# Scores of the 64-feature heads as products of row halves of the array, and small products gathered

## The chip, the cores and the metric

The kernel runs on one NeuronCore of one Trainium2 chip. A time is the device time of one execution in microseconds (us). The profile records one execution. It names the engines PE (TensorE, matrix products) with PEld (its loads of the stationary operand), DVE (VectorE), ACT (ScalarE), POOL (GpSimd) and SP (SyncE, which here issues the loads of weights). The array of TensorE has 128 rows, along which the sum of a product runs, and 128 columns.

## What is computed

`x` is 256 positions by 1024 features, float32. Block 1 runs two layers of FFN1, hybrid mixer and FFN2, each with a residual and a layer norm; block 2 runs two layers of a second mixer. Only the mixers contain what the change touches:

```python
# block 1: hybrid_mixer, head dimension 64
qa, ka, va, qr, kr, vr, gr = jnp.split(x @ w_in, IN_SPLITS, axis=-1)
y_attn = sliding_window_sink_attention(rope(qa), rope(ka), va, sinks)  # 8 query heads, 2 key heads, window 128
y_ret = multiscale_retention(rot(qr), rot(kr) / 8, vr, gr)             # 8 heads, decay per head
return jnp.concatenate([y_attn, y_ret], axis=-1) @ w_out
# block 2: second_block
o_a = mla_attention(qa_nope, qa_rope, ka_nope, ka_rope, va)            # 6 heads, 64+32 features, causal
o_b = dilated_attention(p_qb, p_kb, p_vb, slopes_b)                    # 6 heads, 64 features
o_c = sparse_attention(p_qc, p_kc, p_vc, p_qi, p_ki, p_wi, slopes_c)   # 4 heads, 64 features
#   index score of a key: sum over 8 heads of w * relu(q_idx . k_idx); each query keeps its best 64 keys
sub = (jnp.concatenate([o_a, o_b, o_c], -1) * silu(p_gate)) @ w_out
```

## The kernel before

`program` runs the stages `Ffn1`, `Mixer1`, `Ffn2` twice and `Mixer2` twice. Weights stream once from memory through a ring of six stage buffers on SP's one queue. Every piece is split into a high and a low part (`whi` by a copy on ACT, L300; `wlo` by a subtraction on DVE, L302), and a projection makes three products per 128 features with them (`mm<-whi,xx`, `mm<-wlo,xx`, and transposed, with the activations as what streams, `mm<-xx,whi`). Scores, values and transposes are plain float32; each shows as two records on PE. All matrix products go through the helper `mm` (L331), transposes through `transposes` (L446), and so they are told apart by their tiles: `ac` (four PSUM banks: scores, values, retention), `mm` (two banks: projections), `tr` (two banks: transposes).

**Scores.** The features lie on the rows of the array. A head has 64 features, and the transposed activations hold two heads, one in rows 0 to 63 and one in rows 64 to 127. Before, one operand of each product is a copy padded with zeros in the other head's rows, and the product uses all 128 rows: `kz` (keys of the window attention), `qrz` (queries of the retention), `kiz` (index keys), `kcz` (keys of c), `kbz` (keys of b). POOL fills the zeros, and the two halves are copied by two instructions. Attention a of `Mixer2` has 96 features and uses 96 rows.

**From scores to values.** `softmax` (L657) brings a bank of scores, one (128 x 512) tile of several heads, to `P`: on DVE a scaled addition of the bias (L661), the maximum (L666, L668), small steps for the sinks (L669 to L678), the reciprocal (L679) and in `Mixer1` the product with it (L808); on ACT one exponential per head (L672). `pT` (L682) transposes the blocks of `P` on PE and copies them to `PT` on ACT (L690) or DVE (L692); `av` multiplies them with the values, two heads at a time in column halves of the array (rows of the profile with `128*64`). In the retention, `ret_s` (L839) makes scores of pairs of heads and multiplies them by the decay on DVE (L851, tile `S`); `ret_av` multiplies `S` with the values (`ac<-vr,S`).

**Order.** A scheduler works the order out once, when the kernel is built: it takes the instructions in the order in which the program writes them as their rank, and fixes for each engine one list that the engine works through in order. On the chip a waiting instruction holds back all that stand behind it on its engine. `Mixer1.body` and `Mixer2.body` write scores, transposes, values and projections in alternation, so that a softmax runs on DVE and ACT while PE does a projection. One layer pair has 6 score units of the window attention in `Mixer1` (two of 4 heads x 128 keys, four of 2 heads x 256 keys), 6 of the retention, and in `Mixer2` 5 units of a, 3 of c, 5 of b and two calls of `choose` (the index scores and the selection of keys).

## Time and profile before

| what | value |
|---|---|
| time, median of three runs | 1356.9 us (1353.8, 1356.9, 1357.55) |
| time of the profiled execution | 1357.66 us |
| its span, from first to last instruction | 1355.9 us |
| granted clock of TensorE, mean | 0.997 |
| busy: PE / DVE / ACT / POOL | 98% / 76% / 55% / 3% |
| matrix products (PE records) | 7654 |
| FFN1, `Mixer1`, FFN2 of layer 0 | about 15 to 205, 205 to 306, 306 to 500 us |
| FFN1, `Mixer1`, FFN2 of layer 1 | about 504 to 700, 700 to 802, 802 to 997 us |
| `Mixer2`, layers 0 and 1 | about 997 to 1170, 1178 to 1350 us |

A busy share is the mean over stages with different work. In the timeline a row merges neighbouring instructions of one kind: its start, the time from the first one's start to the last one's end, the engine, the line, what is written and read, the rows*columns of the array for PE, the shape, and the number of records. A PE record's end is modelled and reaches beyond the start of the next, so the time that a group takes is read from its start to the start of what comes behind it. A bracket says for how long the engine stood before the row, and what ended that.

### The profile page before, as it was taken

The page shows a single profiled execution, that of the slowest core. Times are in us where ns is not written, and L with a number is a line of the kernel's source. Part 1 is how long each engine was busy: PE and PEld are TensorE (multiplying, and loading weights), DVE is VectorE, ACT ScalarE, POOL GpSimd, SP SyncE. Part 2 cuts the span into 40 slices and gives each one's busy share as a digit, 9 for nine tenths or more (in the row PEclk, how much of TensorE's full clock was granted, in tenths as well). Part 3 has the DMA queues.
Part 4 walks back from the last instruction along what each step waited for, and adds up shares of the span by engine and source line. Part 5 has one row for each costly group of instructions (what it writes and reads, how often), then busy time and mean ns, then how long its engine had stood idle before and what let it go on. Part 6 is the DMA issues. An engine that isn't in the chain of part 4 may idle for free.

```text
span 1355.9 us, 20444 instructions
## 1 busy us (share of the span) xinstructions
PE 1334.9 (98%) x7654; PEld 1149.7 (85%) x7654; DVE 1035.4 (76%) x1705; ACT 752.2 (55%) x1324; POOL 37.2 (3%) x55
## 2 busy tenths in 40 slices
PE   9999999999999999999999999999999999999997
PEld 7888888888888888878888878888889989799896
DVE  7876769878977669777579778687585796866976
ACT  7655535455654546545445456555355678366691
POOL 0000010010000000000010110000010000000000
PEclk9999999999999999999999999999999999999999
DMA  9987625446877628877433647687445435365320
GB/s 320 343 285 250 218 63 175 154 138 249 310 247 259 218 82 313 282 261 240 147 109 125 209 149 267 204 271 251 129 152 190 144 101 163 127 194 167 121 98 31
DMA packets 75236, 262.89 MB, mean 194 GB/s; under 512 B 9168, under 2 KB 9552, under 8 KB 75008
## 3 DMA queue, kind: packets, MB, share of 16 engines
q1 hardware_dynamic: 74592, 259.82, 57.3%
q0 software_dynamic: 544, 1.75, 0.4%
q8 instruction: 60, 0.98, 0.3%
q14 instruction: 40, 0.33, 0.1%
HBM read 260.49 MB, written 1.05 MB: 193 GB/s over the span
## 4 chain that ended last, share of the span: by engine, by line
PE 82%; DVE 9%; DMA 4%; issue 2%; ACT 2%; POOL 0%; SPq 0%; DVEq 0%; ACTq 0%; POOLq 0%
PE mm L331 39%; PE ac L331 27%; PE tr L331 12%; DMA st<-in_w 4%; PE tr L446 3%; DVE wlo L302 2%; DVE xlo L302 1%; DVE x L411 1%; ACT whi L300 0%; DVE xx L378 0%; DVE ada L317 0%; POOL rs_y L389 0%; DVE bn L414 0%; DVE x L437 0%; DVE x L438 0%
## 5 line engine op out<-in xcount | busy, mean ns | idle before, releaser
L302 DVE TENSOR_TENSOR wlo<-st,whi 128x1024 fp32r<-128x1024 f32 (+4 forms) x319 | 373.1, 1179 | 81.5 <-ACT whi L300 80.4
L300 ACT ACTIVATE whi<-st 128x1024 fp32r<-128x1024 f32 (+4 forms) x319 | 324.0, 1022 | 125.1 <-PE mm L331 57.1
L331 PE MATMUL mm<-xx,whi 128*128 128x256 f32 (+1 forms) x1296 | 334.0, 333 | 0.6 <-ACT whi L300 0.6
L331 PE MATMUL mm<-xx,wlo 128*128 128x256 f32 x928 | 261.2, 282 | 0.0
L331 PEld LDWEIGHTS mm<-xx,whi 128*128 128x128 f32 x1296 | 220.4, 190 | 24.7 <-ACT whi L300 0.9
L331 PE MATMUL mm<-whi,xx 128*128 128x512 f32 (+3 forms) x744 | 220.8, 373 | 0.6 <-DVE xx L378 0.4
L331 PE MATMUL tr<-xx,whi 128*128 128x512 f32 x560 | 195.9, 392 | 0.8 <-ACT whi L300 0.8
L331 PEld LDWEIGHTS mm<-xx,wlo 128*128 128x128 f32 x928 | 176.0, 190 | 2.1 <-DVE wlo L302 0.8
L331 PE MATMUL tr<-xx,wlo 128*128 128x256 f32 x560 | 156.6, 280 | 0.5 <-DVE wlo L302 0.5
L331 PEld LDWEIGHTS mm<-whi,xx 128*128 128x128 f32 x744 | 135.5, 188 | 24.3 <-issue 1.4
L300 ACT ACTIVATE xhi<-st 128x1024 fp32r<-128x1024 f32 x106 | 110.5, 1058 | 74.4 <-PE ac L331 63.0
L302 DVE TENSOR_TENSOR xlo<-st,xhi 128x1024 fp32r<-128x1024 f32 x106 | 128.6, 1220 | 25.2 <-ACT xhi L300 24.4
L331 PE MATMUL mm<-wlo,xx 128*128 128x512 f32 (+3 forms) x372 | 137.9, 371 | 0.0
L331 PE MATMUL ac<-xlo,hth 128*128 128x512 f32 x320 | 126.7, 396 | 0.0
L331 PE MATMUL ac<-xhi,hth 128*128 128x512 f32 x320 | 125.8, 393 | 0.0
L331 PEld LDWEIGHTS tr<-xx,whi 128*128 128x128 f32 x560 | 104.7, 187 | 24.2 <-ACT whi L300 1.1
L331 PEld LDWEIGHTS tr<-xx,wlo 128*128 128x128 f32 x560 | 105.6, 189 | 2.2 <-DVE wlo L302 1.0
L331 PE MATMUL ac<-xhi,htl 128*128 128x512 f32 x320 | 105.5, 394 | 0.0
L317 DVE SCALAR_TENSOR_TENSOR ada<-st,sc,ada 128x1024 f32<-128x1024 f32 x42 | 53.9, 1283 | 37.0 <-DMA st<-in_w 36.7
L331 PEld LDWEIGHTS mm<-wlo,xx 128*128 128x128 f32 x372 | 70.1, 188 | 10.4
L331 PEld LDWEIGHTS ac<-xhi,hth 128*128 128x128 f32 x320 | 60.3, 188 | 14.1
L331 PEld LDWEIGHTS ac<-xhi,htl 128*128 128x128 f32 x320 | 60.2, 189 | 12.4
(286 smaller groups left out, 1890.2 us busy)
## 6 DMA issues: line engine op xcount, KB each, us to landing
st<-in_w SPq DMA_DIRECT2D x442, 512.0 KB, 4.5
st<-in_w SPq DMA_DIRECT2D x20, 384.0 KB, 3.5
g<-in_lng SPq DMA_DIRECT2D x8, 512.0 KB, 4.9
b<-in_lnb SPq DMA_DIRECT2D x8, 512.0 KB, 4.8
st<-in_w SPq DMA_DIRECT2D x8, 432.0 KB, 3.9
st<-in_w SPq DMA_DIRECT2D x8, 296.0 KB, 4.1
st<-in_xT SPq DMA_DIRECT2D x4, 256.0 KB, 3.9
x<-in_x SPq DMA_DIRECT2D x2, 512.0 KB, 6.8
```

What stands on the lines that cost most here:

```text
L300: nc.scalar.activation(out=hi[:, :m], in_=st[:, :m], func=AF.Copy)
L302: nc.vector.tensor_tensor(out=lo[:, :m], in0=st[:, :m], in1=hi[:, :m].bitcast(F32), op=ALU.subtract)
L317: nc.vector.scalar_tensor_tensor(out=self.ada, in0=st, scalar=c, in1=self.ada, op0=ALU.mult, op1=ALU.add)
L331: self.nc.tensor.matmul(*a, **k)
L411: nc.vector.scalar_tensor_tensor(out=x[:, c0:c1], in0=x[:, c0:c1], scalar=alpha, in1=src, op0=ALU.mult, op1=ALU.add)
L446: self.nc.tensor.transpose(ps[:m, 128 * i:128 * i + 128], s, self.idn)
```

## The change

The padded copies and their zeros go. One copy of the whole pair takes the place of two half copies, and each product of a 64-feature head names rows 0 to 63 or rows 64 to 127 for both its operands. The units are made in pairs, one for each row half, into two PSUM banks, and the products of the two halves alternate: in the window attention units 0 and 1, 2 and 4, 3 and 5; in the retention the even and the odd heads; in `choose` the even and odd index heads; in c and b the even and odd heads (`make` with `halves=True`; the units of c are now two, one of 4 heads x 128 keys and one of 4 heads x 256 keys; of b three, the first with 6 heads x 128 keys). Attention a stays in 96 rows. b runs six softmaxes in place of five, c four in place of three, since each bank has its own.

The second part moves work. `together` and `ready` first make the transposes and copies of several units and then the value products of these units in a row; a scheduler's mark (`issue_after`) keeps the products behind the first one of the row. `pT` makes up to four blocks per bank, and its copies alternate between DVE and ACT by a count. The body of `Mixer2` is written in another order, with some of the value products inside and behind the gate projection (`mid`). There are three `PT` buffers in `Mixer2` in place of two. Per layer pair there are nine calls of `together` or `ready`: three in `Mixer1`, six in `Mixer2`.

```diff
+        out = []
+        for i in range(0, len(blocks), 4):
+            bs = blocks[i:i + 4]
+            ps = K.transposes(bs)
+            T = self.scr.tile([128, 512], F32, tag="PT", name="PT", bufs=self.pt_bufs)
+            m = 128 * len(bs)
+            self.n_pt += 1
+            if self.n_pt % 2 == 0:
+                nc.scalar.activation(out=T[:, :m], in_=ps[:, :m], func=AF.Copy)
+            else:
+                nc.vector.tensor_copy(out=T[:, :m], in_=ps[:, :m])
+            out += [T[:, 128 * j:128 * j + 128] for j in range(len(bs))]
+        return out
...
+        fs = [f() for f in steps]
+
+        def products():
+            first = None
+            for f in reversed(fs):
+                with self.K.tc.issue_after(first) if first is not None else nullcontext():
+                    ins = f()
+                first = first if first is not None else ins
+        return products
...
-        self.qT, self.kz = t("qT", [4, 256], self.keep), t("kz", [2, 256])
-        self.qrz, self.krT = t("qrz", [8, 256], self.keep), t("krT", [4, 256], self.keep)
+        self.qT, self.kT = t("qT", [4, 256], self.keep), t("kT", [256])
+        self.qrT, self.krT = t("qrT", [4, 256], self.keep), t("krT", [4, 256], self.keep)
...
+        def score(*two):
+
+            pvs = []
+            for i in two:
+                t, h0, nh, nk = self.attn_units()[i]
+                pvs.append(K.bank("ac", 4)[:, :nh * nk].rearrange("p (h n) -> p h n", h=nh))
...
-            pv = ps[:, :nh * nk].rearrange("p (h n) -> p h n", h=nh)
...
-                h = h0 + j
-                K.mm(pv[:, j, :], lhsT=self.qT[:, h % 4, ts], rhs=self.kz[:, h // 4, :nk], start=True, stop=True)
+                for i, pv in zip(two, pvs):
+                    h = self.attn_units()[i][1] + j
+                    r = slice(64 * (h // 4), 64 * (h // 4) + 64)
+                    K.mm(pv[:, j, :], lhsT=self.qT[r, h % 4, ts], rhs=self.kT[r, :nk], start=True, stop=True)
...
+                t, h0, nh, nk = self.attn_units()[i]
+                p = st.pop(i)
+                nt = nk // 128
+                T = self.pT([p[:, h, 128 * j:128 * j + 128] for h in range(nh) for j in range(nt)])
...
+                        for kt in range(nt):
+                            for e in range(2):
+                                with K.tc.issue_after(first) if first is not None else nullcontext():
+                                    ins = K.mm(y[64 * e:64 * e + 64, c:c + 128], lhsT=self.v[:, kt, 64 * g:64 * g + 64],
+                                               rhs=T[(j + e) * nt + kt], start=kt == 0, stop=kt == nt - 1)
...
+            nc.vector.tensor_copy(out=self.qrT[:, :, ts], in_=ps.rearrange("p (a n) -> p a n", a=4))
...
-            ps = K.bank("ac", 4)
...
-                     start=True, stop=True)
...
+            pvs = [K.bank("ac", 4)[:, :np * nq].rearrange("p (h n) -> p h n", h=np) for _ in range(2)]
+            for j in range(np):
+                for e in range(2):
+                    r = slice(64 * e, 64 * e + 64)
+                    K.mm(pvs[e][:, j, :], lhsT=self.krT[r, p0 + j, 128 * kt:128 * kt + 128], rhs=self.qrT[r, p0 + j, 128 * kt:],
+                         start=True, stop=True)
+            dec = K.dec.rearrange("p (a e n) -> p e a n", e=2, n=256)
+            for e in range(2):
+                P = scr.tile([128, 512], F32, tag="P", name="S", bufs=self.p_bufs)
+                sv = P[:, :np * nq].rearrange("p (h n) -> p h n", h=np)
+                nc.vector.tensor_tensor(out=sv, in0=pvs[e], in1=dec[:, e, p0:p0 + np, :nq], op=ALU.mult)
+                for j in range(np):
+                    S[2 * (p0 + j) + e, kt] = sv[:, j, :]
...
-        score(0)
-        score(1)
+        score(0, 1)
+        score(2, 4)
         self.proj(2, 0, lambda ps: self.rot(ps, 512, 1, 0, "qr"))
-        av(0)
-        score(2)
+        self.together(av(0), av(1))
+        score(3, 5)
         self.proj(2, 1, lambda ps: self.rot(ps, 512, 1, 1, "qr"))
-        av(1)
-        score(3)
         self.proj(3, 0, lambda ps: self.rot(ps, 512, 2, 0, "kr"))
-        av(2)
-        score(4)
+        self.together(av(2), av(4))
         ret_T(0)
         self.proj(3, 1, lambda ps: self.rot(ps, 512, 2, 1, "kr"))
-        av(3)
-        score(5)
+        self.together(av(3), av(5))
         self.proj(4, 0, vcopy(0))
         ret_T(1)
-        av(4)
-        av(5)
         self.proj(4, 1, vcopy(1))
         K.affine(1, self.l, last)
         ret_s(1, 0, 4)
-        ret_s(1, 4, 4)
-        for j in range(4):
-            ret_s(0, 2 * j, 2)
+        ret_s(0, 0, 2)
+        ret_s(0, 2, 2)
...
     p_bufs = 5
-    pt_bufs = 2
+    pt_bufs = 3
...
+        self.kcT, self.kiT = kk[:, 0:2], kk[:, 2]
+        self.kr, self.wi = (kk[:, 3, c:c + 2 * n].rearrange("p (t n) -> p t n", t=2) for c, n in ((0, 32), (64, 8)))
...
-        for h0 in range(0, 8, nh):
-            ps = K.bank("ac", 4)
+        for p0 in range(0, 4, nh):
+            ps = [K.bank("ac", 4) for _ in range(2)]
             for j in range(nh):
-                h = h0 + j
-                K.mm(ps[:, nk * j:nk * j + nk], lhsT=qiT[:, h // 2, 128 * t:128 * t + 128], rhs=self.kiz[:, h % 2, :nk],
-                     start=True, stop=True)
-            rl = self.rl[:, (h0 // nh) % 2]
-            nc.scalar.activation(out=rl, in_=ps, func=AF.Relu, scale=0.125)
-            for j in range(nh):
...
+                for e in range(2):
+                    r = slice(64 * e, 64 * e + 64)
+                    K.mm(ps[e][:, nk * j:nk * j + nk], lhsT=qiT[r, p0 + j, 128 * t:128 * t + 128], rhs=self.kiT[r, :nk],
+                         start=True, stop=True)
...
+            if halves:
+                for p0 in range(0, nh // 2, n):
+                    ps = range(p0, min(p0 + n, nh // 2))
+                    us.append((t, 128 + 128 * t, [[2 * p + e for p in ps] for e in range(2)]))
...
+            t, nk, banks = us[i]
+            pvs = [K.bank("ac", 4)[:, :len(hs) * nk].rearrange("p (h n) -> p h n", h=len(hs)) for hs in banks]
+            for j in range(len(banks[0])):
+                for pv, hs in zip(pvs, banks):
+                    K.mm(pv[:, j, :], lhsT=q(hs[j], slice(128 * t, 128 * t + 128)), rhs=k(hs[j], nk), start=True, stop=True)
...
+                    for h in sorted(ps)[::2]:
...
+                        for kt in range(nt):
+                            for e in range(2):
+                                with K.tc.issue_after(first) if first is not None else nullcontext():
+                                    ins = K.mm(y[64 * e:64 * e + 64, c:c + 128], lhsT=v[:, kt, c + 64 * e:c + 64 * e + 64],
+                                               rhs=T[h + e, kt], start=kt == 0, stop=kt == nt - 1)
+                                first = first if first is not None else ins
...
-                if g == 0:
-                    gated(k)
...
-        a_av(0)
+        self.together(a_av(0), a_av(1))
...
-        a_av(1)
+        a_score(3)
         self.choose(1, self.qiT)
-        a_score(3)
-        a_av(2)
         a_score(4)
-        kbz = scr.tile([128, 6, 256], F32, tag="kT", name="kbz")
-        self.zero_halves(kbz)
-        bv = kbz.rearrange("p (a b) n -> p a b n", b=2)
+        kbT = scr.tile([128, 3, 256], F32, tag="kT", name="kbT")
 
         def post6(b, ps):
             n = 2 - b
-            pv = ps[:, :256 * n].rearrange("p (a n) -> p a n", a=n)
-            self.copy(0, bv[0:64, 2 * b:2 * b + n, 0, :], pv[0:64])
-            self.copy(1, bv[64:128, 2 * b:2 * b + n, 1, :], pv[64:128])
+            self.copy(b, kbT[:, 2 * b:2 * b + n, :], ps[:, :256 * n].rearrange("p (a n) -> p a n", a=n))
 
         self.proj_T(3, post6)
-        a_av(3)
+        self.together(a_av(2), a_av(3))
         c_score(0)
-        a_av(4)
-        c_score(1)
-        c_av(0)
-        c_score(2)
+        b_score, b_av = self.make(6, 0.125, half(qbT), keys(kbT), vb, 5, self.alibi(0, lambda t: self.seg(K.lc, t)), True)
         self.proj(post7)
         K.affine(3, self.l, last)
-        c_av(1)
-        b_score, b_av, nbu = self.make(6, 0.125, lambda h, s: qbT[:, h // 2, s], lambda h, nk: kbz[:, h, :nk],
-                                       vb, 5, self.alibi(0, lambda t: self.seg(K.lc, t)))
-        c_av(2)
+        self.together(a_av(4), c_av(0))
+        c_score(1)
         b_score(0)
+        go = []
+        self.proj_T(4, gpost(0), lambda: go.append(self.ready(c_av(1))))
+        go.pop()()
+        go.append(self.ready(b_av(0)))
         b_score(1)
         b_score(2)
-        b_av(0)
-        b_score(3)
-        b_av(1)
-        b_score(4)
-        self.proj_T(4, gpost(0))
-        b_av(2)
+        gated(0)
+        gated(1)
...
-        self.proj_T(4, gpost(1))
+        go.pop()()
+        self.proj_T(4, gpost(1), lambda: go.append(self.ready(b_av(1), b_av(2))))
...
+        go.pop()()
```

On PE, at the first scores of `Mixer1`, before (`ro`, `rk` are the rotated queries and keys, `P` a softmax):

```order
L446 MATMUL tr<-idn,ro 128x128 x4
L446 MATMUL tr<-idn,rk 128x128
L331 MATMUL ac<-kz,qT 128x128 x8
L331 MATMUL mm<-whi,xx 128x512
L331 MATMUL mm<-wlo,xx 128x512
```

and after:

```order
L446 MATMUL tr<-idn,ro 128x128 x4
L446 MATMUL tr<-idn,rk 128x128
L331 MATMUL ac<-kT,qT 128x128 x8
L331 MATMUL ac<-kT,qT 128x256 x4
L331 MATMUL mm<-whi,xx 128x512 x2
L331 MATMUL mm<-wlo,xx 128x512
```

The first half of the 256-key scores now stands directly behind the 128-key scores.

On DVE, at the same place, before:

```order
L748 COPY kz<-tr 64x128 x2
L661 SCALAR_TENSOR_TENSOR P<-ac,win 128x512
L302 TENSOR_TENSOR wlo<-st,whi 128x1024
L668 TENSOR_REDUCE nm<-P 128x4
L661 SCALAR_TENSOR_TENSOR P<-ac,win 128x512
L669 TENSOR_TENSOR nm<-nm,sink 128x4
L302 TENSOR_TENSOR wlo<-st,whi 128x1024
L670 TENSOR_SCALAR nm<-nm 128x4
L668 TENSOR_REDUCE nm<-P 128x4
L676 TENSOR_TENSOR es<-sink,nm 128x4
```

and after:

```order
L766 COPY kT<-tr 128x128
L302 TENSOR_TENSOR wlo<-st,whi 128x1024
L660 SCALAR_TENSOR_TENSOR P<-ac,win 128x512 x2
L667 TENSOR_REDUCE nm<-P 128x4 x2
L668 TENSOR_TENSOR nm<-nm,sink 128x4
L660 SCALAR_TENSOR_TENSOR P<-ac,win 128x512
L669 TENSOR_SCALAR nm<-nm 128x4
L668 TENSOR_TENSOR nm<-nm,sink 128x4
L667 TENSOR_REDUCE nm<-P 128x2
L675 TENSOR_TENSOR es<-sink,nm 128x4
```

The steps of the two first softmaxes and of a third one (over two heads) now alternate, with no weight split between them.

On PE, at the retention (`krT`, `vr` are its keys and values), before:

```order
L446 MATMUL tr<-idn,P 128x128 x4
L331 MATMUL ac<-qrz,krT 128x128 x6
L331 MATMUL ac<-PT,v 64x128 x4
L331 MATMUL ac<-qrz,krT 128x128 x2
L331 MATMUL ac<-qrz,krT 128x256 x8
L331 MATMUL ac<-vr,S 128x64 x6
L331 MATMUL mm<-whi,xx 128x512
L331 MATMUL ac<-vr,S 128x64 x2
```

and after:

```order
L331 MATMUL mm<-whi,xx 128x512
L331 MATMUL ac<-qrT,krT 128x128 x8
L331 MATMUL ac<-qrT,krT 128x256 x8
L331 MATMUL ac<-vr,S 128x64 x5
L331 MATMUL mm<-whi,xx 128x512
L331 MATMUL mm<-wlo,xx 128x512
L331 MATMUL mm<-whi,xx 128x512
L331 MATMUL ac<-vr,S 128x64 x3
```

The 16 scores now stand in one row, with no window values between them.

On PE, at c and b in `Mixer2` (`vc` are the values of c, `va` those of a, `kk` holds the keys of c and of the index), before:

```order
L331 MATMUL ac<-PT,vc 64x128 x4
L331 MATMUL ac<-kbz,qbT 128x128 x3
L446 MATMUL tr<-idn,P 128x128 x2
L331 MATMUL ac<-kbz,qbT 128x128
L446 MATMUL tr<-idn,P 128x128 x2
L331 MATMUL ac<-kbz,qbT 128x128 x2
L331 MATMUL ac<-kbz,qbT 128x256
L331 MATMUL ac<-PT,vc 64x128 x4
L331 MATMUL ac<-kbz,qbT 128x256
L331 MATMUL mm<-xx,whi 128x256
```

and after:

```order
L331 MATMUL mm<-xx,whi 128x256 x2
L331 MATMUL mm<-xx,wlo 128x256
L331 MATMUL ac<-PT,vc 64x128 x4
L331 MATMUL ac<-PT,va 64x128 x4
L331 MATMUL ac<-kk,qcT 128x256 x4
L331 MATMUL ac<-kbT,qbT 128x128 x6
L331 MATMUL mm<-xx,whi 128x256 x2
```

Four kinds of small work that alternated stand in two rows: values, then scores.

## Rows read from the trace of the kernel before

**Rows 1.** The page: the span, and the busy time of each engine.

```profile
span 1355.9 us, 20444 instructions
...
PE 1334.9 (98%) x7654; PEld 1149.7 (85%) x7654; DVE 1035.4 (76%) x1705; ACT 752.2 (55%) x1324; POOL 37.2 (3%) x55
```

**Rows 2.** Windows: stretch; length; busy us of PE, PEld, DVE, ACT, POOL; clock, DMA.

```profile
215.00:260.00 45.00, 44.98 (x248) 35.96 (x247) 42.97 (x87) 25.49 (x61) 0.00 (x0) 1.00 0.50 161
...
1074.00:1122.00 48.00, 47.19 (x354) 42.69 (x353) 46.64 (x126) 36.10 (x93) 1.47 (x2) 1.00 0.37 123
1122.00:1140.00 18.00, 18.00 (x150) 16.73 (x149) 9.39 (x15) 17.19 (x34) 0.00 (x0) 1.00 0.36 119
```

**Rows 3.** Timeline of PE: the first scores of Mixer1, and what follows them.

```profile
214.33 1.95 PE L331 MATMUL ac<-kz,qT 128*128 128x128 f32 x16
...
216.04 0.47 PE L331 MATMUL mm<-whi,xx 128*128 128x512 f32 x1
```

**Rows 4.** Timeline of PE: the index scores of both halves, and what follows each.

```profile
1064.70 1.95 PE L331 MATMUL ac<-kiz,qiT 128*128 128x128 f32 x16
1066.40 0.36 PE L331 MATMUL mm<-xx,wlo 128*128 128x256 f32 x1
...
1080.65 3.72 PE L331 MATMUL ac<-kiz,qiT 128*128 128x256 f32 x16
1084.21 1.03 PE L331 MATMUL ac<-kaT,qaT 96*128 96x256 f32 x4
```

**Rows 5.** Timeline of PE: values in column halves, between whole-array products.

```profile
227.74 0.40 PE L331 MATMUL mm<-wlo,xx 128*128 128x512 f32 x1
...
228.07 0.66 PE L331 MATMUL ac<-PT,v 128*64 128x128 f32 x8
...
228.66 1.13 PE L331 MATMUL ac<-kz,qT 128*128 128x256 f32 x4
...
229.63 0.60 PE L446 MATMUL tr<-idn,P 128*128 128x128 f32 x4
```

**Rows 6.** Timeline of PE: projection products, one behind the other.

```profile
258.43 0.62 PE L331 MATMUL mm<-whi,xx 128*128 128x512 f32 x2
258.89 0.39 PE L331 MATMUL mm<-wlo,xx 128*128 128x512 f32 x1
```

**Rows 7.** Timeline of DVE: steps one behind the other, then the two first softmax ends.

```profile
217.16 0.68 DVE L668 TENSOR_REDUCE nm<-P 128x4 f32<-128x512 f32 x1
...
217.76 0.68 DVE L661 SCALAR_TENSOR_TENSOR P<-ac,win 128x512 f32<-128x512 f32 x1
...
218.36 0.15 DVE L669 TENSOR_TENSOR nm<-nm,sink 128x4 f32<-128x4 f32 x1
218.43 1.22 DVE L302 TENSOR_TENSOR wlo<-st,whi 128x1024 fp32r<-128x1024 f32 x1
...
219.56 0.16 DVE L670 TENSOR_SCALAR nm<-nm 128x4 f32<-128x4 f32 x1
...
224.94 0.69 DVE L808 TENSOR_TENSOR P<-P,rd 128x512 f32<-128x512 f32 x1
...
227.41 0.68 DVE L808 TENSOR_TENSOR P<-P,rd 128x512 f32<-128x512 f32 x1
```

**Rows 8.** Timeline of PE: transposes of the first softmax of Mixer1.

```profile
225.92 0.60 PE L446 MATMUL tr<-idn,P 128*128 128x128 f32 x4
```

**Rows 9.** Timeline of PE: end of the retention.

```profile
261.80 4.17 PE L331 MATMUL ac<-qrz,krT 128*128 128x128 f32 x20
265.81 1.45 PE L331 MATMUL ac<-vr,S 128*128 128x64 f32 x12
267.06 0.48 PE L331 MATMUL mm<-whi,xx 128*128 128x512 f32 x1
```

**Rows 10.** Timeline of DVE: one of the six decay products of the retention.

```profile
263.42 0.69 DVE L851 TENSOR_TENSOR S<-ac,dec 128x512 f32<-128x512 f32 x1 [0.17 <-PE ac L331]
```

**Rows 11.** Timeline of PE: a wait for copied transposes in Mixer2.

```profile
1086.68 0.66 PE L331 MATMUL ac<-PT,va 128*64 128x128 f32 x8 [0.29 <-ACT PT L690]
```

More of the change, by code (lines that the diff above doesn't have):

```diff
@@ L745, in qk_T @@
         ps = K.transposes([self.ro["k", t][:, 0:128]])
[L746 to L748 removed]
+        nc.vector.tensor_copy(out=self.kT[:, ts], in_=ps[:, 0:128])
     def first(self, t, g):
@@ L1068, in make @@
+    def make(self, nh, scale, q, k, v, k0, bias, halves):
         K, nc = self.K, self.K.nc
[L1069 to L1070 removed]
+        us = self.units(nh, halves)
         st, yps = {}, {}
         def score(i):
[L1074 to L1082 removed]
```

243 lines of the change are left out of this document (109 added, 134 removed).

## The prediction

> **What bounds the kernel now.** I read the page first, for which engine has no idle time; then the busy time by windows over the mixers, since the change touches nothing else; then PE's timeline at each kind of product that changes; and last the rows of DVE there, because DVE makes the operands that PE takes next. The page shows PE busy for 1334.9 of 1355.9 us [rows 1], so the time is what PE has to do, plus 21 us of start, end and waits. In the two stretches with most of the small products PE is busy for 44.98 of 45.0 us and 47.19 of 48.0 us. But DVE is busy for 42.97 and 46.64 us of the same stretches, so only 2.0 and 1.4 us are free on it, while it has 9.39 of 18 us behind the second one [rows 2]. A microsecond taken from PE counts there only if DVE can follow. The granted clock is 1.00 in all these stretches [rows 2].
>
> A unit's price comes from starts, since ends are modelled. Sixteen records of 128 columns run from 214.33 to 216.04: 1.71 us, 0.107 each, eight products [rows 3]. The index scores give 1.70 us for the same shape and, for eight products of 256 columns, 3.56 us, of which about 0.11 is the step into the group: 3.45 us, or 0.216 a record [rows 4]. A projection product of 512 columns takes 0.23 us [rows 6].
>
> **The change part by part.**
>
> *Row halves.* Two products of 64 rows that run beside each other take the time of one. In `Mixer1` the window scores are 8 products of 128 and 8 of 256 columns, the retention the same: 2 x (1.71 + 3.45) = 10.3 us, so 5.15 us go. In `Mixer2` the index is one such set (5.15 us), c half of one (2.6), b three quarters (3.9): 11.6 us, of which 5.8 go. Per layer pair 10.95, for two 21.9 us. No product of row halves stands in the trace. The nearest are the values, in column halves: eight records in 0.59 us (228.07 to 228.66), where one behind the other they would take 0.86 [rows 5]. So halves do run abreast for float32, and I take the full halving; the other end, no gain, stays a rival.
>
> *Changes of kind.* Whole-array and halved products don't mix freely. Around the values, 227.74 + 0.23 is 227.97, but they start at 228.07: 0.10. Inside, 0.59 instead of 4 x 0.107 = 0.43: 0.16. Behind, four records of 256 take 0.97 us, not 0.86: 0.11 [rows 5]. A visit costs 0.37 us. `Mixer1` makes 6 before (values) and 5 after plus one step from one kind of halves to the other; `Mixer2` 11 before, 10 after plus two such steps. A step between kinds is not in the trace; between nothing and a whole visit (0.37) I take 0.37, the row at hand. Sum: nothing to 0.4 us per mixer in either direction; I take none.
>
> *What DVE gives back in Mixer1.* The first softmax ends now at 224.94 + 0.6, and PE takes its transposes at 225.92 [rows 7, 8], with 43 projection products between scores and transposes. After the change PE has there the 128-key scores (0.86 us), four products of 256 columns (0.86) and 32 projection products (7.4), and comes to the transposes at about 223.4. DVE's list up to the first finished `P` has four bias additions and four maxima at 0.60, one weight split at 1.13, thirteen small steps at 0.07, and three parts of a rotation and the last product, some 1.5 together (an estimate from the same widths) [rows 7]: 8.4 us. It starts behind a weight split at about 216.1, so `P` is there at about 224.6: PE stands 1.2 us. In the retention PE saves 2.58, but six decay products at 0.60 us need 3.6 us, and with four `ac` banks the scores can't run far ahead; now they wait for PE by 0.17 us each [rows 10], at 0.86 us of scores per product. 16 records of 256 columns and 12 values then take about 3.9 of the 5.26 us of now (261.80 to 267.06) [rows 9], with the 128-column part about 1.5 us of gain: 1.05 given back. Mixer1: 5.15 - 1.2 - 1.05 = 2.9 us.
>
> *What DVE gives back in Mixer2.* The second pair of index banks in `choose` waits for banks that two scores of a now hold, until DVE has read both: about 0.9 us, as the scores of PE get ahead by half of 3.45 and DVE takes 2 x 0.60 to free them. c has four softmaxes in place of three: 0.9 for its extra pass over a half bank with its small steps (0.35 + 0.33 + 0.2). b's sixth softmax moves, with two units, behind the gate projection, where DVE has 8.6 of 18 us free [rows 2]; I take 0.5 for it. Waits for transposes that are copied late, such as the 0.29 us [rows 11], go with the gathering; they add 0.3. Mixer2: 5.8 - 0.9 - 0.9 - 0.5 + 0.3 = 3.8 us.
>
> *At nothing.* The memsets leave POOL, which is busy 37 us in all [rows 1]; nobody waits for it. One copy for two half copies frees DVE and ACT for less than 1 us per mixer, counted in the list above. One weight load passes loads of layer-norm constants on SP's queue; the ring holds six pieces, which cover it. If the cover were gone, a load's lateness would show as a DMA wait ahead of `whi`.
>
> *The sum.* 2 x (2.9 + 3.8) = 13.4 us. The profiled execution took 1357.66 us, 0.76 above the median of the runs: 1357.66 - 13.4 - 0.76 = 1343.5, about **1344**. Its ends: with nothing given back and 1.5 us of waits gone, 21.9 + 1.5 = 23.4 us, 1333.5; with half of the Mixer1 gain lost and three quarters of that of Mixer2, 2 x (1.45 + 0.95) = 4.8 us, 1352.
>
> **The rivals.**
>
> *DVE becomes the bound* in the stretches where it has 2.0 and 1.4 us free [rows 2]. Then a layer pair gains 3.4 us: 6.8 in all, 1350. For it: DVE works its list in order, and the new list puts four softmaxes where two stood. Against: weight splits can run ahead, since the ring is filled before the mixer, and DVE has half of its time free behind each stretch. The Trainium skill, "TensorEngine Tiling (Array Packing)", section "PSUM Bottleneck", warns of just this: packing makes products faster, but not the reading of their banks by other engines. Rows 2 agree as to the room that is left.
>
> *Loads of the two halves go one behind the other.* Products that stream only 64 columns take 1.25 / 12 = 0.104 us each [rows 9], as long as those of 128: there the load of the 128-column stationary operand sets the pace. If two row halves load in turn, 0.107 each, a pair of 128-column products takes 0.21, as before, and only the 256-column ones gain. The 128-column part of the saving is 1.7 in Mixer1 and (1.70 + 0.85 + 1.28) / 2 = 1.9 in Mixer2, 7.3 in all; 14.6 of 21.9 remain, and with the same share given back 8.9 us: 1348. The values don't decide it, as their loads are half as wide. The Trainium skill, "TensorE: Matmul & The Clock Gate", section "LDWEIGHTS (loading the stationary operand)", has the load's time go by columns whatever the rows, which speaks for this rival; its page "TensorEngine Tiling (Array Packing)", "Key Properties", lets different tiles load and multiply in parallel, which speaks against. No row here settles it.
>
> *Row halves don't run abreast at all.* Then PE has the work of before, and the change of order is about neutral: 1357. Against it: the column halves do [rows 5].
>
> *The gathering makes PE stand* (slower than before). Value products wait until the last of their units is transposed and copied, and nothing else on PE may pass. The two first softmaxes end 2.47 us apart [rows 7], and PE has eight projection products, 1.84 us, between their transposes: 0.6 short. If a weight split (1.13 with its step, 1.22 at most) stands on DVE ahead of the last one, each gathered place costs 0.6 + 1.22 = 1.8 us. There are 18; break-even is 21.9 / 18 = 1.2 us each. 18 x 1.8 = 33 us: 1357.66 - 21.9 + 33 - 0.76 = 1368. For it: DVE has next to no room. Against: the list was fixed with these waits in view, and four of nine places stand in or behind a projection with microseconds of products ahead of them on PE.
>
> **How the numbers follow.** Forecast 0.55; DVE as the bound 0.20; loads in turn 0.12; no halves abreast 0.05; gathering too dear 0.08. About 0.3% (4 us) is what a measurement can tell from no change. The range takes in the first three, with the forecast's two ends: 1333 to 1353; the two that stay out have 0.13. Faster by over 0.3% (below 1352.8): the forecast and nearly all of the second and third, 0.81. Within 0.3%: no halves abreast and the upper edges, 0.11. Slower: 0.08.
>
> **What would show it.** Row halves: the first scores of `Mixer1` take 0.86 us from their start to the next group, and index scores of 256 columns about 1.8; 1.7 and 1.8 mean loads in turn; 1.7 and 3.5 mean that they don't run abreast. DVE: PE rows with a bracket that names DVE at transposes of `P` and at the values behind `S`, with DVE's busy time near the length of those stretches. Gathering: waits of over 1 us ahead of `PT,v`, `PT,va` and `PT,vc`, or ahead of the transposes. The feed-forward stages should last as long as before; a prediction that fails there was wrong on what else the change moves.

## The result and the profile after

The changed kernel takes 1346.0 us (median of seven runs, 1341.55 to 1350.96), against 1356.65 us for the kernel before: a ratio of 0.9918 with the interval 0.9896 to 0.9941, 10.7 us less. The forecast was 1344. The gain is put together otherwise than the forecast had it, which the stages and the experiments below show. The profiled run is the slowest of the seven.

The page of the changed kernel, the profiled run of 1350.96 us; these lines answer to [rows 1]:

```profile
span 1349.2 us, 20437 instructions
...
PE 1319.8 (98%) x7654; PEld 1135.5 (84%) x7654; DVE 1031.4 (76%) x1713; ACT 741.4 (55%) x1310; POOL 25.8 (2%) x35
```

PE is busy for 15.1 us less, not for 21.9, and its share has not moved. Where the time went is read stage by stage. The table has the length of each stage in one profiled execution, from the start of the last gathering of statistics of one layer norm (DVE, line L415) to that of the next, the first from the span's start, in us; the kernels of the last three rows are experiments below.

| kernel | FFN1 0 | Mixer1 0 | FFN2 0 | FFN1 1 | Mixer1 1 | FFN2 1 | Mixer2 0 | Mixer2 1 |
|---|---|---|---|---|---|---|---|---|
| before | 195.8 | 113.4 | 189.9 | 191.6 | 115.0 | 188.6 | 181.1 | 174.2 |
| changed | 199.8 | 109.7 | 190.4 | 189.3 | 112.1 | 188.6 | 178.9 | 173.9 |
| `whole` | 196.2 | 112.2 | 189.9 | 189.4 | 112.9 | 188.6 | 178.5 | 172.9 |
| `apart` | 196.8 | 109.8 | 190.7 | 189.6 | 109.0 | 188.6 | 179.1 | 174.1 |
| `blater` | 196.9 | 110.2 | 190.6 | 189.6 | 109.6 | 188.6 | 178.4 | 171.7 |

The feed-forward stages differ by what single executions differ by: the 4 us in the first stage stand in the stretch in which the first weights arrive, and the change does not touch it. In this one execution Mixer1 gained 3.7 and 2.9 us; Mixer2 2.2 and 0.3. The second layer of either has a stand of PE in it that is shown below.

**The halves run abreast.** Timeline of PE: the first scores of Mixer1, which answer to [rows 3] (now 8 products of 128 columns and 4 of 256 in one group), and the index scores, which answer to [rows 4].

```profile
217.68 2.03 PE L331 MATMUL ac<-kT,qT 64*128 64x128 f32 x24
219.64 0.73 PE L331 MATMUL mm<-whi,xx 128*128 128x512 f32 x2
...
1060.23 1.16 PE L331 MATMUL ac<-kk,qiT 64*128 64x128 f32 x16
1061.32 0.39 PE L331 MATMUL mm<-xx,wlo 128*128 128x256 f32 x1
...
1076.10 1.56 PE L331 MATMUL ac<-kk,qiT 64*128 64x256 f32 x10
1078.18 1.13 PE L331 MATMUL ac<-kk,qiT 64*128 64x256 f32 x6 [0.53 <-DVE P L660]
1079.24 1.13 PE L331 MATMUL ac<-kaT,qaT 96*128 96x256 f32 x4
```

From start to start, the 24 records take 1.96 us, where one behind the other they took 3.33 (`whole`, below). The index scores of 128 columns take 1.09 us in place of 1.70. Those of 256 columns take 3.14 us in place of 3.56 (3.45 without the entry), since PE stands in their middle: the second pair of banks waits for DVE to read a softmax of a.

**Mixer1 as forecast.** Timelines at the first transposes of a softmax (PE) and at the retention (PE, then DVE), which answer to [rows 7 to 10].

```profile
227.71 0.63 PE L446 MATMUL tr<-idn,P 128*128 128x128 f32 x4 [0.52 <-DVE es L675]
...
261.43 2.03 PE L331 MATMUL ac<-qrT,krT 64*128 64x128 f32 x24
263.85 1.72 PE L331 MATMUL ac<-qrT,krT 64*128 64x256 f32 x8 [0.40 <-DVE S L878]
265.51 1.33 PE L331 MATMUL ac<-vr,S 128*128 128x64 f32 x10
```

```profile
263.12 3.67 DVE L878 TENSOR_TENSOR S<-ac,dec 128x512 f32<-128x512 f32 x6
```

PE comes to the first transposes before the softmax is done. In the retention the six decay products stand on DVE without a gap, 3.67 us for six, where each waited for PE by 0.17 us before.

**A new wait in Mixer2.** The timelines of ACT and PE in its second layer, at the scores of b (`y` is the copy that frees a bank, `qiTw` the high part of a weight for the output projection):

```profile
1283.29 1.06 ACT L300 ACTIVATE qiTw<-st 128x1024 fp32r<-128x1024 f32 x1 [2.31 <-DMA st<-in_w]
1284.26 0.81 ACT L1042 ACTIVATE y<-ac 128x128 f32<-128x128 f32 x3
```

```profile
1282.05 1.13 PE L331 MATMUL ac<-kk,qcT 64*128 64x256 f32 x8
1284.73 1.31 PE L331 MATMUL ac<-kbT,qbT 64*128 64x128 f32 x12 [1.54 <-ACT y L1042]
...
1286.75 0.63 PE L331 MATMUL mm<-xx,whi 128*128 128x256 f32 x2
1287.17 0.41 PE L331 MATMUL mm<-xx,wlo 128*128 128x256 f32 x1
...
1289.74 0.40 PE L331 MATMUL mm<-xx,whi 128*128 128x256 f32 x2
1289.98 0.28 PE L331 MATMUL mm<-xx,wlo 128*128 128x256 f32 x1
```

PE stands for 1.54 us. It waits for two banks; ACT has to copy one of them out, and in ACT's list a weight split stands ahead of that copy, and it waits for its transfer. Behind the stand, two projection products take 0.42 us from start to start (1286.75 to 1287.17), and 0.24 us a little later (1289.74 to 1289.98): for some 3 us the clock is at its lower level, 1.2 GHz. The windows show it as 0.83 over 10 us:

```profile
1280.00:1290.00 10.00, 7.99 (x62) 6.96 (x61) 10.00 (x25) 7.69 (x23) 0.00 (x0) 0.83 0.57 184
```

**A stand that was there before.** The second Mixer1 of this run has one of the same kind ahead of its first scores (ACT, then PE; `qT` is the copy of the transposed queries):

```profile
707.09 1.06 ACT L300 ACTIVATE whi<-st 128x1024 fp32r<-128x1024 f32 x1 [2.15 <-DMA st<-in_w]
708.06 0.58 ACT L764 ACTIVATE qT<-tr 128x512 f32<-128x512 f32 x1
```

```profile
708.69 0.33 PE L446 MATMUL tr<-idn,rk 128*128 128x128 f32 x1 [2.01 <-ACT qT L764]
708.94 3.60 PE L331 MATMUL ac<-kT,qT 64*128 64x128 f32 x24
712.47 0.78 PE L331 MATMUL mm<-whi,xx 128*128 128x512 f32 x2
```

The scores behind the stand take 3.53 us where the same 24 records took 1.96 in the first layer, and the granted clock from 710 to 720 us is 0.87. The kernel before stands at the same place, with the granted clock at 1.00 behind:

```profile
710.21 0.66 PE L446 MATMUL tr<-idn,ro 128*128 128x128 f32 x4 [2.06 <-ACT qT L744]
```

So the 115.0 and 112.1 us of the second Mixer1 each hold a late transfer that the kernel before has too (in `whole` PE stands there for 0.90 us, in `apart` for less than 0.4), and the first Mixer1 is the cleaner measure: 113.4 before, 112.2 in `whole`, 109.7 in the changed kernel.

### The profile page after: what moved, and what is told of

Read it like the earlier page. It is cut to its first block, busy times and chain, and to the rows that moved or that the text cites. A ratio compares the mean times of both kernels' runs of the same rounds, so it can differ in the third digit from the quotient of the medians.

```text
span 1349.2 us, 20437 instructions
## 1 busy us (share of the span) xinstructions
PE 1319.8 (98%) x7654; PEld 1135.5 (84%) x7654; DVE 1031.4 (76%) x1713; ACT 741.4 (55%) x1310; POOL 25.8 (2%) x35
## 5 line engine op out<-in xcount | busy, mean ns | idle before, releaser
L300 ACT ACTIVATE xhi<-st 128x1024 fp32r<-128x1024 f32 x106 | 110.2, 1056 | 67.6 <-PE ac L331 56.3
```

The source lines that it names most:

```text
L300: nc.scalar.activation(out=hi[:, :m], in_=st[:, :m], func=AF.Copy)
```

## The experiments

Times are medians in us, beside the kernel before on the same chip; "the changed kernel" is 1346.0 throughout. The kernel before took 1356.65 us in the round of the changed kernel and 1355.07 to 1355.74 in those of the experiments, so a difference of 1 to 2 us between medians of different rounds may be the round's. Several kernels compute other scores or leave work out, as their expectations say.

**1. `whole`: the same order, products of 128 rows.** This separates the halves from the rest of the change, since every engine's list is the same.

```diff
-                    r = slice(64 * (h // 4), 64 * (h // 4) + 64)
+                    r = slice(0, 128)
...
-                    r = slice(64 * e, 64 * e + 64)
+                    r = slice(0, 128)
...
-        half = lambda x: lambda h, s: x[64 * (h % 2):64 * (h % 2) + 64, h // 2, s]
+        half = lambda x: lambda h, s: x[:, h // 2, s]
```

> The order of the changed kernel on every engine, but each 64-feature product uses all 128 rows again (both operands whole, so a score is the sum of two heads' scores). Theory H, the row halves make the gain because they halve the work of PE: PE has 21.9 us more to do than in the changed kernel, the waits for DVE that the changed kernel shows shrink or go, and the time is that of the kernel before within 3 us, 1354 to 1360. Theory G, the new order and the copies and memsets that went make it: within 3 us of the changed kernel, 1343 to 1349. Between them: the difference to 1346 is the share of the halves, the difference to 1356.7 that of the order.

Measured: 1349.1 (1347.79 to 1353.58, eleven runs) against 1355.07; ratio 0.9962 (0.9947 to 0.9977). It lies between the two theories. By the medians, 6.0 us of the gain are there with no halves at all, and the halves add 3.1; by the ratios, each to the kernel before in its own round, it is 5.1 and 6.0. So the rest of the change (the order, with the copies and zeros that went) makes 5 to 6 us and the halves 3 to 6; which of the two makes more is not shown. Timeline of PE, `whole`, the same places as above:

```profile
214.28 3.68 PE L331 MATMUL ac<-kT,qT 128*128 128x128 f32 x24
217.61 0.58 PE L331 MATMUL mm<-whi,xx 128*128 128x512 f32 x1
...
1075.92 3.75 PE L331 MATMUL ac<-kk,qiT 128*128 128x256 f32 x16
1079.50 1.03 PE L331 MATMUL ac<-kaT,qaT 96*128 96x256 f32 x4
```

The first scores take 3.33 us, not 1.96; the index scores 3.58, without a wait in their middle. What the order alone gives can be counted. Each step between whole products, column halves and row halves costs PE about 0.19 us (half of the 0.37 of a visit). The trace of before has 12 such steps in a Mixer1 and 22 in a Mixer2, `whole` has 6 and 14, the changed kernel 11 and 22. So the steps of `whole` come to 2 x (6 + 8) x 0.19 = 5.3 us less, near to what it gained; and the halves, which bring steps of their own, take these back. That is a count at one price, and no run changes the steps alone.

**2. `apart`: first all products of the lower half, then all of the upper.**

```diff
             for j in range(nh):
-                for i, pv in zip(two, pvs):
...
+            for i, pv in zip(two, pvs):
+                for j in range(nh):
```

> As the changed kernel, with row halves, but of each pair of banks first all products of the lower half, then all of the upper half. If two products run abreast only when a product of the other half stands next to it (theory H): no saving but at the one border in each group, so PE works nearly as in the kernel with whole products, and steps between kinds of products come on top: 1356 to 1362. If the array keeps both halves busy whatever the order: 1343 to 1349. The first scores of Mixer1 (8 products of 128 columns) would take about 1.6 us, or 0.9 to 1.0.

Measured: 1345.5 (1340.38 to 1351.38) against 1355.07; ratio 0.9928 (0.9906 to 0.9951), as the changed kernel. The time does not tell, but the groups do. Timelines of PE, the second scores of Mixer1 (four lower and four upper records), `apart` and then the changed kernel:

```profile
229.74 1.14 PE L331 MATMUL ac<-kT,qT 64*128 64x256 f32 x8
230.81 0.50 PE L331 MATMUL mm<-whi,xx 128*128 128x512 f32 x1
```

```profile
232.73 1.13 PE L331 MATMUL ac<-kT,qT 64*128 64x256 f32 x8
233.79 0.50 PE L331 MATMUL mm<-whi,xx 128*128 128x512 f32 x1
```

1.07 and 1.06 us: nothing is lost. Where eight lower records stand ahead of eight upper ones it is otherwise. The first scores of Mixer1 and the index scores of 128 columns in `apart`:

```profile
214.70 2.58 PE L331 MATMUL ac<-kT,qT 64*128 64x128 f32 x24
217.21 0.73 PE L331 MATMUL mm<-whi,xx 128*128 128x512 f32 x2
...
1054.87 1.71 PE L331 MATMUL ac<-kk,qiT 64*128 64x128 f32 x16
1056.51 0.39 PE L331 MATMUL mm<-xx,wlo 128*128 128x256 f32 x1
```

They take 2.51 us, where the changed kernel needs 1.96 and `whole` 3.33; and 1.64, where the changed kernel needs 1.09 and the kernel before 1.70. There alternating is worth 0.55 us a group. The kernel is no slower for it; one thing that speaks for PE having had room is that the changed kernel's wait of 0.53 us for the second pair of index banks is not there in the first Mixer2 of `apart`.

**3. `ungathered`: each unit's values right behind its own transposes.**

```diff
-        self.ready(*steps)()
+        for f in steps:
+            f()()
```

> As the changed kernel, but the value products of a unit stand right behind its own transposes in the program, not in a row with those of the next unit. If gathering is worth its saved visits of the halved mode (up to 6 per layer pair at 0.37 us): 1346 to 1350. If gathering costs more in waits than it saves (theory of the fourth rival, weak): 1340 to 1344. No difference within 2 us: the scheduler's list already puts them together.

Measured: 1342.9 (1341.27 to 1343.96) against 1355.07; ratio 0.9908 (0.9895 to 0.9922). It lies in the range of the second answer (gathering costs more than it saves), but the intervals overlap: gathering by hand gains nothing, and that it costs 3 us is not shown. The scheduler's list keeps most of the values together anyway: the steps between kinds are 11 in Mixer1, as with gathering, and 24 instead of 22 in Mixer2.

**4. `m1only`: Mixer1 as changed, Mixer2 (and its helpers) as before.**

```diff
-class Mixer2(OutProj, Attn):
+class Attn0:
...
+class Mixer2(OutProj, Attn0):
```

`Attn0` and this `Mixer2` are the two classes of the kernel before.

> Mixer1 as changed, Mixer2 as before. The stages of the two traces say that a Mixer1 gains 3.9 and 2.9 us, so 1356.7 - 6.8 = 1350; my sum said 2.9 each, 1351. If Mixer2 makes most of the gain, as my sum had it (3.8 each): 1350 to 1353; if Mixer1 makes nearly all: 1346 to 1348.

Measured: 1346.9 (1345.09 to 1348.48) against 1355.07; ratio 0.994 (0.9927 to 0.9953). Mixer1 makes 8.1 us of the gain, the third answer; in its own trace the two Mixer1 stages last 110.3 and 109.4 us.

**5. `relief`: less work on DVE.**

```diff
-                nc.vector.tensor_tensor(out=p, in0=p, in1=rd.unsqueeze(2).to_broadcast([128, nh, nk]), op=ALU.mult)
+                for j in range(nh):
+                    nc.scalar.activation(out=p[:, j, :], in_=p[:, j, :], func=AF.Copy, scale=rd[:, j:j + 1])
...
-                                  self.alibi(6, lambda t: self.sel[t]), True)
+                                  lambda t, hs, nk: self.sel[t].unsqueeze(1).to_broadcast([128, len(hs), nk]), True)
```

> The changed kernel with less work on DVE: in Mixer1 the last product of each softmax goes to ACT (one copy with a scale per head), in Mixer2 the 20 tables of the distance bias of b and c are left out (the bias is the mask alone, so these scores are others). Theory D, DVE's list is the bound in both mixers: some 3.6 us less on DVE per Mixer1 and 5 to 6 us per Mixer2 take 1.5 to 2 us and 3 to 6 us off each, 1331 to 1337. Theory B, the waits come from the four banks and from ACT, not from DVE's load: at most 3 us in all, 1342 to 1346.

Measured: 1353.3 (1347.31 to 1358.91, twelve runs) against 1355.74; ratio 0.9984 (0.9968 to 1.0001). Neither theory: slower than the changed kernel by 7. The two mixers have to be told apart. In Mixer2, where the tables are left out and nothing is put elsewhere, the windows over its small products are clear; `relief`, the changed kernel, `whole`, each 100 us (busy us of PE, PEld, DVE, ACT):

```profile
1050.00:1150.00 100.00, 96.78 (x764) 88.59 (x762) 78.88 (x179) 76.39 (x173) 0.00 (x0) 1.00 0.42 138
```

```profile
1050.00:1150.00 100.00, 97.08 (x752) 87.53 (x751) 83.15 (x191) 77.20 (x172) 0.00 (x0) 1.00 0.41 138
```

```profile
1050.00:1150.00 100.00, 99.50 (x751) 92.50 (x751) 82.87 (x192) 76.93 (x172) 0.00 (x0) 1.00 0.42 138
```

DVE has 4.3 us less to do, and PE is not busier. Mixer2 0 lasts 178.9 us with and without, so DVE's load is not what holds it. Mixer2 1 falls from 173.9 to 171.2; there the wait for `y` and the slow clock behind it are gone, as in kernels that keep DVE's work (experiments 3 and 8). In Mixer1 the relief does not answer the question, as it changes the order: DVE's list now has a weight split ahead of the last two decay products, the split waits for ACT, which got the softmax's work, and PE stands. Timelines of DVE and PE in `relief`:

```profile
264.17 1.23 DVE L302 TENSOR_TENSOR wlo<-st,whi 128x1024 fp32r<-128x1024 f32 x1 [1.69 <-ACT whi L300]
265.31 1.28 DVE L879 TENSOR_TENSOR S<-ac,dec 128x512 f32<-128x512 f32 x2
```

```profile
266.05 0.69 PE L331 MATMUL ac<-vr,S 128*128 128x64 f32 x2 [1.80 <-DVE S L879]
```

The granted clock is 0.66 from 265 to 275 us, and Mixer1 0 lasts 114.4 us.

**6. `whole_relief`: the same relief with products of 128 rows.**

```diff
-                    r = slice(64 * e, 64 * e + 64)
+                    r = slice(0, 128)
...
-                nc.vector.tensor_tensor(out=p, in0=p, in1=rd.unsqueeze(2).to_broadcast([128, nh, nk]), op=ALU.mult)
+                for j in range(nh):
+                    nc.scalar.activation(out=p[:, j, :], in_=p[:, j, :], func=AF.Copy, scale=rd[:, j:j + 1])
```

> The same two reliefs of DVE in the kernel with whole 128-row products. Theory D: there PE is the bound, so relief brings little, 1345 to 1349, and the row halves are now worth 10 to 16 us (against some 3.5 without relief). Theory B: the halves are worth the same with and without relief, 3 to 5 us.

Measured: 1353.3 (1349.58 to 1355.27) against 1355.74; ratio 0.9979 (0.9969 to 0.999). By the medians the halves are worth nothing with relief, so theory D falls; the 3 to 5 us of theory B are not there either. `relief` has the stand in Mixer1 that was shown, so the pair is no clean measure of the halves. The stages of Mixer2 here (179.2 and 172.3 us) are those of `whole` within 0.7.

**7. `un_both`: a candidate** (not gathered, softmax's last product on ACT, distance tables on POOL in two steps).

```diff
-                self.K.nc.vector.scalar_tensor_tensor(out=w[:, j, :], in0=self.seg(self.K.dist, t), scalar=s, in1=base(t),
-                                                      op0=ALU.mult, op1=ALU.add)
+                g = self.K.nc.gpsimd
+                g.tensor_scalar(out=w[:, j, :], in0=self.seg(self.K.dist, t), scalar1=s, scalar2=None, op0=ALU.mult)
+                g.tensor_tensor(out=w[:, j, :], in0=w[:, j, :], in1=base(t), op=ALU.add)
```

> A candidate for a better kernel: not gathered, the last product of the Mixer1 softmaxes on ACT, and the tables of the distance bias made on POOL in two steps (a scaling and an addition) in place of one on DVE. Theory D: 1331 to 1338. If POOL's two steps are so slow that the softmaxes of b and c wait for them: 1343 to 1352, with waits that name POOL.

Measured: 1363.9 (1361.25 to 1366.9) against 1355.74; ratio 1.0064 (1.005 to 1.0077), slower than the kernel before and above both ranges. In its trace DVE's bias additions wait for POOL's tables six times, 10.8 us in all, and PE waits 8.6 us for transposes' operands that ACT scales last.

**8. `blater`: the first scores of b in the middle of the gate projection.**

```diff
-        b_score(0)
         go = []
-        self.proj_T(4, gpost(0), lambda: go.append(self.ready(c_av(1))))
+        def mid0():
+            b_score(0)
+            go.append(self.ready(c_av(1)))
+        self.proj_T(4, gpost(0), mid0)
...
-        go.append(self.ready(b_av(0)))
...
+        def mid1():
+            self.together(b_av(0))
+            go.append(self.ready(b_av(1), b_av(2)))
+        self.proj_T(4, gpost(1), mid1)
```

> The changed kernel with the first scores of b moved from ahead of the gate projection into its middle, and the first values of b behind them into the second gate projection. The trace of the changed kernel has PE wait 0.6 and 1.7 us there for two banks that ACT still reads, and in the second layer the granted clock is at its lower level for 3 us behind that wait. If this wait is the loss: 3 to 4 us less than the changed kernel, 1342 to 1343, and no slow clock in Mixer2. If DVE's list is the bound, the wait turns up later: 1345 to 1347.

Measured: 1343.6 (1342.18 to 1345.88) against 1355.74; ratio 0.9914 (0.9902 to 0.9927), 2.4 below the changed kernel, a little short of what the wait should give. Mixer2 1 falls from 173.9 to 171.7 us, and the wait for `y` and the slow clock behind it are gone. Mixer2 0, which had the shorter wait, falls by 0.5 only: there PE stands for the same time at transposes and copies further on.

**9. `m1half`: row halves in Mixer1 alone**, Mixer2 with 128 rows.

```diff
-                    r = slice(64 * e, 64 * e + 64)
+                    r = slice(0, 128)
...
-        half = lambda x: lambda h, s: x[64 * (h % 2):64 * (h % 2) + 64, h // 2, s]
+        half = lambda x: lambda h, s: x[:, h // 2, s]
```

Both places are in `Mixer2`.

> The changed kernel with row halves in Mixer1 alone; in Mixer2 the products of the index, of c and of b use all 128 rows in the same order (so their scores are sums of two heads'). The stages say that halves save 3 us in a Mixer1 and nothing in a Mixer2. If so: the kernel with whole products (1349.1) less 6, 1342 to 1345, no slower than the changed kernel. If the halves of Mixer2 are worth as much as those of Mixer1: 1348 to 1352.

Measured: 1346.2 (1344.49 to 1347.4) against 1355.27; ratio 0.9925 (0.9909 to 0.994). It lies between the two ranges. It is 2.9 below `whole` (5.0 by the ratios) and 0.2 above the changed kernel: the halves of Mixer1 give 3 to 5 us, those of Mixer2 nothing that these medians can tell.

**10. `nord`: Mixer2 without the scaling of each softmax on ACT.**

```diff
-                for j in range(n):
-                    nc.scalar.activation(out=v[:, j, :], in_=v[:, j, :], func=AF.Copy, scale=rd[:, j:j + 1])
```

> The changed kernel without the scaling by the reciprocal of the sum on ACT in Mixer2 (left out: the weights of a, b and c stay unscaled), which is 2 to 4 instructions of 0.3 to 0.4 us in each softmax, between its exponentials and its transposes. Theory L, what takes the gain back in Mixer2 is the length of each chain from scores to copied transposes, for which PE has less to do meanwhile: 1 us less per chain, 5 places per Mixer2, so 3 to 4 us less per Mixer2 and 1336 to 1340 in all. If it is the room of the four banks: 1343 to 1346.

Measured: 1342.2 (1340.6 to 1344.38) against 1355.27; ratio 0.9898 (0.9882 to 0.9914). That lies between the two ranges, 3.8 below the changed kernel, but the stages say that it isn't shorter chains: Mixer2 0 lasts 178.7 us against 178.9, and Mixer2 1 171.1, as `blater` and `ungathered` have it (171.7, 171.1), which keep all the work. Theory L falls as well.

**11 and 12. `un_blater` and `blater_pt`: two candidates.**

The first is the edit of 3 and that of 8 together. The second has the edit of 8 and, in `Mixer2`, a fixed engine for the copies:

```diff
-            if self.n_pt % 2 == 0:
+            if (self.n_pt % 2 == 0 if self.pt_act is None else self.pt_act):
...
+        self.pt_act = True
         self.together(a_av(0), a_av(1))
...
+        self.pt_act = False
         self.together(a_av(4), c_av(0))
```

> Candidate: values not gathered, and the first scores of b in the middle of the gate projection. Each alone gave 1342.9 and 1343.6. If both take away waits of their own: 1339 to 1342; if they only keep PE from standing so long that its clock falls: 1342 to 1344, as each alone.

Measured: 1343.7 (1342.53 to 1349.38) against 1355.27; ratio 0.9916 (0.9898 to 0.9934): the two edits don't add up.

> Candidate: the first scores of b in the middle of the gate projection, and in Mixer2 the copies of transposes by a fixed choice, ACT for those of a up to the scores of c (where DVE is busy all the time) and DVE behind that (where ACT is), in place of taking turns. If the engine of the copy is what PE waits for at the values (0.6 us twice in each Mixer2): 1340 to 1342. If the chain ahead of the copy is: 1342 to 1345.

Measured: 1342.8 (1339.99 to 1345.1) against 1355.27; ratio 0.9902 (0.9885 to 0.992). It lies in the second range (the chain ahead of the copy), though within 1 us of the first. With `ungathered` it is the fastest that computes the reference, some 3 us below the changed kernel; the intervals overlap, so neither is shown to beat it.

## Why the prediction was right, and where its steps were not

*The number.* 1344 was forecast, 1346 measured; the range and the sign held. By the stages, a Mixer1 gained about 4 us (113.4 before, without the late transfer of the second layer; 108.9 to 110.3 in the kernels with halves and an unchanged softmax, but for the 112.1 with its stand), and a Mixer2 2.2 and 0.3, where the sum had 2.9 and 3.8. The two errors nearly cancel, so that the number came so close is in part luck.

*Row halves.* Right: products of the two halves take half the time, at either width, so the 21.9 us do go from PE's products, less the steps that the halves bring. The forecast took this from column halves and had no row of row halves; it held. The rival with loads in turn is refuted by the 128-column index scores: 1.09 us, of which some 0.2 are steps between kinds, where it had 1.7. The Trainium skill, "TensorEngine Tiling (Array Packing)", section "Key Properties", says that different tiles can load and multiply in parallel; this case's trace agrees, with the 1.09 us. That no halves run abreast is refuted by the same rows.

*Changes of kind.* This is the step that failed, though not in its sum. It weighed the visits saved against those added, found them even, and so took the new order for neutral. The count is even (12 and 22 steps before, 11 and 22 after), but it hides two terms of opposite sign: the change without halves is worth 5 to 6 us (`whole`), and by the count the row halves' own steps cost that much of what they save. Nothing was the right sum of the two; that the new order is neutral was wrong, and the rival "no halves abreast" would by that have been about 1350, not 1357.

*What comes back in Mixer1.* Right in kind and place. At the first transposes PE stood 0.5 us by the bracket where 1.2 was forecast; the retention, from its first score to the first value product, takes 4.08 and 3.59 us in the two layers, 1.2 and 1.7 less than the 5.24 of `whole`, where 1.5 was forecast. The halves' gain of 5.15 ends as 2.5 to 3.

*What comes back in Mixer2.* Right at one place: the wait for the second pair of index banks was put at 0.9 us, and PE stands there for 0.53 by the bracket, 0.7 by the distance of the records (0.90 in place of 0.21). Under-sized as a whole (the 0.9 for c and the 0.5 for b were not read by themselves): halves take 5.8 us from PE, and the stage is no shorter than that of `whole`. Of the 5.8, eight more steps between kinds are 1.5 (8 x 0.19). Much of the rest goes in waits of 0.4 to 1.5 us at nearly every place where PE takes up a softmax or a bank: PE's idle time in the stage is 3.3 and 3.6 us in the two layers, and 0.8 in `whole`. In the first layer half of it ends by DVE and half by ACT. That is 2.5 to 2.8 us; the last 1.5 to 2 are not attributed.

*DVE as the bound.* The rival read DVE's busy time, 46.6 of 48 us, as having no room. `relief` took 4.3 us of it away in Mixer2, and the first one stayed as long, so an almost full engine was not the bound. What the traces show in its place is the coupling of in-order lists: a weight split on ACT that waits for a transfer holds up the copy that frees a bank, and PE stands for the bank. `blater` moves that one and gets 2 us in Mixer2 1; taking work off the chains (`nord`) or off DVE (`relief`) gets none in Mixer2 0. In Mixer2 1 the changed kernel and `apart`, whose profiled runs have a stretch at the lower clock there, take 173.9 and 174.1 us; `ungathered`, `relief`, `blater` and `nord`, which have none, take 171.1 to 171.7. So some 2 us of what the changed kernel lost in that stage go with the slow clock; without it the stage is 1.2 and 1.8 us below the 172.9 of `whole` in `blater` and `ungathered`, which do all the work.

*What stays open.* Which change would let PE have the 4 us or so that each Mixer2 gives back is not settled. Neither DVE's load nor ACT's scaling is the cause by itself, and an order in which fewer places wait was not found. Nor is it shown why `ungathered` and `blater` are some 3 us below the changed kernel in the median. Their granted clock is 0.997 or 0.998 in every run; the changed kernel's three shortest runs have 0.998 to 0.999 and take 1341.6 to 1343.5, as these two, and its four longest have 0.994 to 0.996 and take 1346.0 to 1351.0. The profiled run of the changed kernel, its slowest, has three stands (2.25, 2.01 and 1.54 us) with a slow clock behind each, and `blater`'s profiled run has no slow clock in these places; that such stands make the difference in the other runs fits their clocks, but no other run of it has a profile.

*Gathering.* The rival that gathering makes PE stand was wrong by far in size (33 us), and right in that gathering brings nothing: without it the kernel is not slower.

## What to carry to other kernels

Where a change has two parts, cost the second one too: here the order of small products, which was taken for neutral, was worth about as much as the halves, and a kernel with the same order and the old products told them apart. PE time that is taken from a stage in which scores, softmax and values alternate turns to waits unless the chains around it get more cover; look for an instruction that waits for a transfer ahead of a copy that frees a bank on the same in-order engine. A busy share near one does not make an engine the bound; take some of its work away before believing it.

## What the runs showed of the hardware that was not expected

Products of the two row halves need not alternate to run abreast, if few stand in a row. In `apart`, with four records of the lower half ahead of the first one of the upper, the upper's first record starts 0.014 us after the lower's first. With eight lower records ahead (the first scores of Mixer1), the upper's first starts together with the lower's fifth, 0.55 us behind the first. In both, the record that starts early stands four places behind the one beside it. So the order is free in the short group (1.07 against 1.06 us), and in the long one it is not (2.51 against 1.96 us).

A stand of PE can cost more than its length. In the profiled run of the changed kernel, a stand of 2.25 us at 12.9 us, when the first weights arrive, is followed by products at half speed:

```profile
15.16 0.73 PE L331 MATMUL tr<-xx,whi 128*128 128x512 f32 x2 [2.25 <-ACT whi L300]
...
17.01 0.63 PE L331 MATMUL tr<-xx,whi 128*128 128x512 f32 x1
17.44 0.41 PE L331 MATMUL tr<-xx,wlo 128*128 128x256 f32 x1
17.65 0.63 PE L331 MATMUL tr<-xx,whi 128*128 128x512 f32 x1
```

and the granted clock of the 20 us from 15 on is 0.91; stand and slow clock are what the first stage of this run lost to the kernel before, and no part of the change. The stands of 2.01 and 1.54 us shown above are followed by the lower clock too, and the stand of 2.06 us of the kernel before is not, so the length of a stand alone does not tell.
